# Issuing half of the memory keys' transfers from Scalar's queue in a one-core hybrid decoder layer

## The chip, the cores and the metric

The kernel runs as one program on one core of a Trainium2 chip. The metric is the device time of one execution in microseconds (us). A core has a TensorE (PE in the profile, with its weight loads as PEld), a VectorE (DVE), a ScalarE (ACT), a GpSimd (POOL) and a SyncE (SP). All of them run their own instruction rows in order and meet through semaphores. A transfer between the chip's memory and the on-chip buffers is issued by an instruction that stands in one of these rows (here SP's or ACT's) and is then carried out by the core's 16 DMA engines.

## The reference, cut to what matters

The reference computes one decoder layer for 512 prompt rows and for 8 samples of 4 rows: a mixer of two kinds of heads, a cross-attention into 256 memory tokens, and a gated MLP with a short convolution. The change touches the samples' cross-attention, whose keys and values come from a cache in memory:

```python
def mem_attend(h, mk, mv, w_mq, w_mo):
    B, T, _ = h.shape
    q = (h @ w_mq).reshape(B, T, MEM_HEADS, MEM_HEAD_DIM)
    s = jnp.einsum('bqhd,bkhd->bhqk', q.astype(jnp.float32), mk.astype(jnp.float32)) * (MEM_HEAD_DIM ** -0.5)
    p = jax.nn.softmax(s, axis=-1)
    o = jnp.einsum('bhqk,bkhd->bqhd', p, mv.astype(jnp.float32)).reshape(B, T, D_MODEL)
    return o.astype(h.dtype) @ w_mo
...
mem_attend(h, cache_mem_k[l], cache_mem_v[l], ...)   # samples: 8 x 256 tokens x 4 heads x 256, float32
```

## The kernel before

All products are float32 accuracy made of three passes: a number is split into a high part (a cast on ACT, L146) and the rest (a subtraction on DVE, L147), for weights (`wslot`, loaded through a staging tile `wst`) and activations alike.

The stretch around the change works as follows. The queries' projection (weights `w_mq`) makes eight chunks of 128 columns, numbered 0 to 7 here. Chunks 0 to 3 come first (L1428): the first halves of the four, then their second halves; chunks 4 to 7 follow (L1556), both halves of a chunk together. Each half is one PSUM tile `mm`, from a pool of five. It is emptied by ACT (`qh`, L1420), then DVE (`ql`, L1421), and a second half, which holds the samples' 32 columns, once more by ACT (`qs`, L1423); only then may TensorE take its buffer again. POOL spreads `qs` into `qx` (L1408).

Beside this, `mk_load` (L1488 to L1494) fetches a sample's memory keys: two tiles of 128 partitions per sample (c = 0, 1), each by four transfers, one a head, of 32 partitions and 128 KB. The eight samples make 64 transfers, 8.4 MB. Three samples of the first four use six staging tiles (`wst`), shared with the weights of the chunks 4 to 7; the others use weight slots or a free tile (`kvt`). `mk_turn` (L1498) lets DVE transpose each tile once its four transfers have landed. After all chunks, TensorE does part of the prompt's cross-attention (`sca`, L1441), the samples' scores (`ssc`, L1510) from `qx` and the transposed keys, and turns the prompt's softmax (`cpt`, L1459), which needs the softmax's last step on DVE (`cp`, L1450). The samples' values come after that (L1538).

The order on every engine is made by a scheduler when the program is built; so a change in one line can move instructions on several engines. Transfers use eight completion counters (DMAHW0 to DMAHW7 in the rows below), handed out in turn in the program's order whatever the queue: an issue waits until the transfer that held its counter before has landed. An instruction that waits holds up all that stands behind it in its engine's row, and that holds for a transfer's issue too.

Of the kernel before, what the change touches and what calls it, by code (L numbers as in the profile page):

```python
# [20 lines left out]
NS = NB * TS  # L21
# [56 lines left out]
def kernel(ctx: ExitStack, tc: tile.TileContext, I, O):  # L78
    nc = tc.nc
# [47 lines left out]
    def v2(t, b):  # L127
        return t.rearrange("p (a b) -> p a b", b=b)
# [10 lines left out]
    dma = nc.sync.dma_start  # L139
# [1070 lines left out]
    for b in range(4):  # L1210
        c = slice(b * P, b * P + P)
# [3 lines left out]
    kst, kts, pts, aTs, outs, rcs = {}, {}, {}, {}, {}, {}  # L1215
# [260 lines left out]
    kst, vts = {}, {}  # L1476
# [4 lines left out]
    def two(i):  # L1481

        if i < 3:
            return [stage(), stage()]
        t = wp.tile([P, 2, DM], F32, name="kvt", tag="W") if i < 7 else S([P, 2, DM], F32, "kvt")
        return [t[:, 0], t[:, 1]]

    def mk_load(b):  # L1488

        kst[b] = two(home[b])  # L1490
        for c in range(2):
            for h in range(H):
                dma(out=v2(kst[b][c][NS * h:NS * h + NS], 256),
                    in_=I["cache_mem_k"][0, b, c * P:(c + 1) * P, h].rearrange("(k t) d -> t k d", t=NS))  # L1494

    def mk_turn(b):
# [57 lines left out]
    for k in range(4):  # L1554
        mk_load(SEQS[k])
    for i, _ in enumerate(gemmB(hqT, [ev_q(m) for m in range(4, 8)])):  # L1556
        if i % 4 == 1:
            mk_turn(SEQS[i // 4])
        if i % 4 == 3:
            mk_load(SEQS[4 + i // 4])  # L1560
# [424 lines left out]
```

## Time and profile before

| | us |
|---|---|
| runs of the kernel | 952.9, 953.73, 956.4 (median 953.73) |
| profiled execution, whole | 950.42 |
| its span, first to last instruction | 948.6 |
| TensorE matmul busy in the span | 918.3 (97%) |
| DVE busy | 606.2 (64%) |
| ACT busy | 377.7 (40%) |

Times in the rows are microseconds from the span's start. A row of the timeline gives start, duration, engine and source line, what is written and read, how many instructions are merged (x), and in brackets how long the engine had been idle and which instruction or transfer ended that. A row on SPq or ACTq is the issue of a transfer, not the transfer. A row of the windows gives a stretch, its length, busy time and count of instructions of the five engines, the granted TensorE clock (1.00 is full), the busy share of the DMA engines, and GB/s moved.

### The profile page before, as it was taken

The page shows a single profiled execution, that of the slowest core. Times are in us where ns is not written, and L with a number is a line of the kernel's source. Part 1 is how long each engine was busy: PE and PEld are TensorE (multiplying, and loading weights), DVE is VectorE, ACT ScalarE, POOL GpSimd, SP SyncE. Part 2 cuts the span into 40 slices and gives each one's busy share as a digit, 9 for nine tenths or more (in the row PEclk, how much of TensorE's full clock was granted, in tenths as well). Part 3 has the DMA queues.
Part 4 walks back from the last instruction along what each step waited for, and adds up shares of the span by engine and source line. Part 5 has one row for each costly group of instructions (what it writes and reads, how often), then busy time and mean ns, then how long its engine had stood idle before and what let it go on. Part 6 is the DMA issues. An engine that isn't in the chain of part 4 may idle for free. (4 is left out here: it accounts for less than half of the span.)

```text
span 948.6 us, 17140 instructions
## 1 busy us (share of the span) xinstructions
PE 918.3 (97%) x6612; PEld 800.8 (84%) x6612; DVE 606.2 (64%) x1120; ACT 377.7 (40%) x727; POOL 202.6 (21%) x401
## 2 busy tenths in 40 slices
PE   8999999999999999988989999999999999999995
PEld 5899787889866778988767899989988997999974
DVE  6845145565886358576544778638757775676767
ACT  5655234344676357613434532322212222222232
POOL 6610000115432226301000544001110110110114
PEclk9999999999999999999989999999999999999998
DMA  8950023344870539999744733062053313512023
GB/s 285 309 183 2 2 88 137 89 139 131 280 245 9 176 103 343 262 192 260 273 175 124 208 126 89 25 174 72 8 142 100 102 27 92 153 49 89 24 93 116
DMA packets 127586, 130.30 MB, mean 137 GB/s; under 512 B 9336, under 2 KB 95193, under 8 KB 127505
## 3 DMA queue, kind: packets, MB, share of 16 engines
q1 hardware_dynamic: 121320, 125.70, 43.8%
q10 hardware_dynamic: 6184, 3.52, 1.2%
q8 instruction: 52, 0.85, 0.4%
q14 instruction: 30, 0.24, 0.1%
HBM read 112.26 MB, written 16.93 MB: 136 GB/s over the span
## 5 line engine op out<-in xcount | busy, mean ns | idle before, releaser
L485 PE MATMUL mm<-fT,wslot 128*128 128x256 f32 x1872 | 235.9, 288 | 0.0
L485 PEld LDWEIGHTS mm<-fT,wslot 128*128 128x128 f32 x1872 | 234.4, 188 | 1.8 <-issue 0.8
L146 ACT CAST wslot<-wst 128x1024 fp32r<-128x1024 f32 x125 | 130.7, 1050 | 256.7 <-issue 71.8
L147 DVE TENSOR_TENSOR wslot<-wst,wslot 128x1024 fp32r<-128x1024 f32 x125 | 155.2, 1246 | 83.3 <-ACT wslot L146 82.8
L1795 PE MATMUL mm<-wslot,act 128*128 128x512 f32 (+1 forms) x180 | 70.2, 391 | 0.0
L1796 PE MATMUL mm<-wslot,act 128*128 128x512 f32 (+1 forms) x180 | 70.0, 392 | 0.0
L1794 PE MATMUL mm<-wslot,act 128*128 128x512 f32 (+1 forms) x180 | 69.3, 387 | 0.0
L1700 POOL COPY cvo<-u 128x2 f32<-128x2 f32 x43 | 10.4, 243 | 204.0 <-DVE u L1698 194.0
L411 PE MATMUL mm<-wslot,hT 128*128 128x512 f32 x128 | 51.3, 402 | 0.0
L485 PE MATMUL mm<-hT,wslot 128*128 128x256 f32 (+1 forms) x384 | 51.0, 289 | 0.0
L413 PE MATMUL mm<-wslot,hT 128*128 128x512 f32 x128 | 51.0, 399 | 0.0
L412 PE MATMUL mm<-wslot,hT 128*128 128x512 f32 x128 | 50.8, 397 | 0.0
L1695 DVE TENSOR_TENSOR u<-mm,rsb 128x256 f32<-128x256 f32 x43 | 18.1, 423 | 50.1 <-PE mm L485 50.1
L485 PEld LDWEIGHTS mm<-hT,wslot 128*128 128x128 f32 x384 | 49.2, 188 | 0.5 <-issue 0.2
L1794 PEld LDWEIGHTS mm<-wslot,act 128*128 128x128 f32 x180 | 34.3, 191 | 8.0 <-issue 0.8
L1796 PEld LDWEIGHTS mm<-wslot,act 128*128 128x128 f32 x180 | 33.8, 188 | 7.3 <-issue 0.4
L1795 PEld LDWEIGHTS mm<-wslot,act 128*128 128x128 f32 x180 | 33.8, 188 | 7.2
L1712 ACT ACTIVATE c<-c 128x560 f32<-128x560 f32 x21 | 14.1, 672 | 57.0 <-DVE c L1706 57.0
L1706 DVE SCALAR_TENSOR_TENSOR c<-u,cvT,c 128x560 f32<-128x560 f32 x43 | 34.3, 797 | 0.9
L1705 DVE SCALAR_TENSOR_TENSOR c<-u,cvT,c 128x560 f32<-128x560 f32 x43 | 34.1, 793 | 0.2
L1807 DVE TENSOR_TENSOR yp<-mm,yp 128x512 f32<-128x512 f32 (+1 forms) x41 | 27.2, 674 | 5.2 <-PE mm L1796 5.1
L485 PE MATMUL mm<-hqT,wslot 128*128 128x256 f32 x192 | 26.2, 299 | 3.8 <-ACT qs L1423 3.8
(482 smaller groups left out, 1828.4 us busy)
## 6 DMA issues: line engine op xcount, KB each, us to landing
wst<-in_w_up_dram SPq DMA_DIRECT2D x42, 512.0 KB
wst<-in_w_in_dram SPq DMA_DIRECT2D x28, 512.0 KB
wst<-in_w_down_dram SPq DMA_DIRECT2D x20, 512.0 KB
kvt<-in_cache_mem_k_dram SPq DMA_DIRECT2D x40, 128.0 KB
kvt<-in_cache_mem_v_dram SPq DMA_DIRECT2D x10, 512.0 KB
wst<-in_w_mk_dram SPq DMA_DIRECT2D x8, 512.0 KB
xb<-in_x_prompt_dram SPq DMA_DIRECT2D x8, 512.0 KB
wst<-in_cache_dk_dram SPq DMA_DIRECT2D x16, 256.0 KB
```

The lines of the kernel that those rows point to most:

```text
L146: nc.scalar.copy(out=hi, in_=src)
L147: (eng or nc.vector).tensor_tensor(out=lo, in0=src, in1=f32(hi), op=SUB)
L411: mm(ps[b], lhsT=xt.hi(k, c0, c0 + n), rhs=s[:, 0, kk, :], start=(k == 0), stop=False)
L412: mm(ps[b], lhsT=xt.hi(k, c0, c0 + n), rhs=s[:, 1, kk, :], start=False, stop=False)
L413: return mm(ps[b], lhsT=xt.lo(k, c0, c0 + n), rhs=s[:, 0, kk, :], start=False, stop=(k == nk - 1))
L485: mm(ps[i], lhsT=s[:, l, k, :], rhs=x(k, c0, c1), start=(k == 0 and j == 0), stop=(k == 7 and j == 2))
L1705: STT(out=c, in0=u[:, 1:EXT - 1], scalar=w[1], in1=c, op0=MUL, op1=ADD)
L1706: STT(out=c, in0=u[:, 0:EXT - 2], scalar=w[0], in1=c, op0=MUL, op1=ADD)
L1794: mm(ps, lhsT=t[:, 0, c0:c0 + P], rhs=s[:, 0, i % 2, cs], start=st, stop=False)
L1795: mm(ps, lhsT=t[:, 0, c0:c0 + P], rhs=s[:, 1, i % 2, cs], start=False, stop=False)
L1796: return mm(ps, lhsT=t[:, 1, c0:c0 + P], rhs=s[:, 0, i % 2, cs], start=False, stop=en)
L1807: VTT(out=y, in0=ps, in1=y, op=ADD)
```

## The change

```diff
         kst[b] = two(home[b])
         for c in range(2):
             for h in range(H):
-                dma(out=v2(kst[b][c][NS * h:NS * h + NS], 256),
+                (dma, nc.scalar.dma_start)[h % 2](out=v2(kst[b][c][NS * h:NS * h + NS], 256),
                     in_=I["cache_mem_k"][0, b, c * P:(c + 1) * P, h].rearrange("(k t) d -> t k d", t=NS))
```

`dma` is SP's `dma_start`. Of every four transfers of a tile, those of heads 0 and 2 stay in SP's row, those of heads 1 and 3 go into ACT's. What is moved, how much, and where it lands stay as they were; 32 of the 64 issues change their row. TensorE's and POOL's orders are the same as before.

The first place is ACT's row where the second tile of values' weights is split (`mvN`), the first halves of chunks 2 and 3 are emptied (`qh`), and the weights of chunk 4 are cast (`wslot`). Names in brackets are the semaphores that an instruction waits for. Before:

```order
L146 CAST mvN<-wst 128x1024 [waits DMAHW2_49]
L1420 ACTIVATE qh<-mm 128x256 [waits DMAHW6_49,PE_49]
L1420 ACTIVATE qh<-mm 128x256 [waits PE_49]
L146 CAST wslot<-wst 128x1024 [waits DMAHW3_49,PE_49]
L1420 ACTIVATE qh<-mm 128x256
```

The same place on ACT now:

```order
L146 CAST mvN<-wst 128x1024 [waits DMAHW2_49]
L1493 DMA kvt<-in_cache_mem_k_dram 32x4x256
L1420 ACTIVATE qh<-mm 128x256 [waits DMAHW6_49,PE_49]
L1493 DMA wst<-in_cache_mem_k_dram 32x4x256 [waits DMAHW4_49,DVE_49]
L1493 DMA wst<-in_cache_mem_k_dram 32x4x256 [waits DMAHW6_49]
L1420 ACTIVATE qh<-mm 128x256 [waits PE_49]
L1493 DMA wst<-in_cache_mem_k_dram 32x4x256 [waits DMAHW0_49,DVE_49]
L1493 DMA wst<-in_cache_mem_k_dram 32x4x256 [waits DMAHW2_49]
L1493 DMA kvt<-in_cache_mem_k_dram 32x4x256 [waits DMAHW4_49]
L1493 DMA kvt<-in_cache_mem_k_dram 32x4x256 [waits DMAHW6_49]
L146 CAST wslot<-wst 128x1024 [waits DMAHW3_49,PE_49]
L1420 ACTIVATE qh<-mm 128x256
```

Eight issues (one more stands just ahead of these rows) have come in front of the cast of chunk 4's weights. The fourth of them takes its counter from the last of the four weight transfers of `w_mq` (DMAHW6), and the eighth takes its counter from the fourth.

The second place is ACT's row for the chunks 4 to 7, where before only the emptying of PSUM stood. Before, from chunk 4 to chunk 7:

```order
L1420 ACTIVATE qh<-mm 128x256 x2
L1423 ACTIVATE qs<-mm 128x32
L1420 ACTIVATE qh<-mm 128x256 x2
L1423 ACTIVATE qs<-mm 128x32
L1420 ACTIVATE qh<-mm 128x256 x2
L1423 ACTIVATE qs<-mm 128x32
L1420 ACTIVATE qh<-mm 128x256 x2
L1423 ACTIVATE qs<-mm 128x32
```

Now, from the `qs` of chunk 4 to the issues ahead of the `qs` of chunk 7:

```order
L1423 ACTIVATE qs<-mm 128x32
L1493 DMA kvt<-in_cache_mem_k_dram 32x4x256 x2
L1420 ACTIVATE qh<-mm 128x256 x2
L1493 DMA kvt<-in_cache_mem_k_dram 32x4x256 x3
L1423 ACTIVATE qs<-mm 128x32
L1493 DMA kvt<-in_cache_mem_k_dram 32x4x256
L1420 ACTIVATE qh<-mm 128x256 x2
L1493 DMA kvt<-in_cache_mem_k_dram 32x4x256 x2
L1423 ACTIVATE qs<-mm 128x32
L1493 DMA kvt<-in_cache_mem_k_dram 32x4x256 x2
L1420 ACTIVATE qh<-mm 128x256 x2
L1493 DMA kvt<-in_cache_mem_k_dram 32x4x256 x2
```

Behind the `qs` of chunks 4, 5 and 6 now stand two, one and two issues; they belong to the second tile (c = 1) of a sample, which DVE transposes before it does the next chunk's `ql`. The `qs` of chunk 7 and two last issues, for the last tile of all, follow these rows.

The third place is DVE's row from the low part of chunk 4's weights (the first `wslot`) to the `ql` of chunk 2's second half. Before:

```order
L147 TENSOR_TENSOR wslot<-wst,wslot 128x1024
L1421 SCALAR_TENSOR_TENSOR ql<-mm,qh 128x256
L1498 STREAM_TRANSPOSE wst<-wst 128x1024 x2
L1498 STREAM_TRANSPOSE kvt<-kvt 128x1024
L147 TENSOR_TENSOR wslot<-wst,wslot 128x1024
L1421 SCALAR_TENSOR_TENSOR ql<-mm,qh 128x256
L1498 STREAM_TRANSPOSE kvt<-kvt 128x1024
L1498 STREAM_TRANSPOSE wst<-wst 128x1024
L147 TENSOR_TENSOR wslot<-wst,wslot 128x1024
L1421 SCALAR_TENSOR_TENSOR ql<-mm,qh 128x256
```

The same place on DVE now:

```order
L1498 STREAM_TRANSPOSE kvt<-kvt 128x1024
L147 TENSOR_TENSOR wslot<-wst,wslot 128x1024
L1421 SCALAR_TENSOR_TENSOR ql<-mm,qh 128x256
L1498 STREAM_TRANSPOSE wst<-wst 128x1024
L147 TENSOR_TENSOR wslot<-wst,wslot 128x1024
L1498 STREAM_TRANSPOSE wst<-wst 128x1024
L1421 SCALAR_TENSOR_TENSOR ql<-mm,qh 128x256
L1498 STREAM_TRANSPOSE kvt<-kvt 128x1024
L1498 STREAM_TRANSPOSE wst<-wst 128x1024
L147 TENSOR_TENSOR wslot<-wst,wslot 128x1024
L1421 SCALAR_TENSOR_TENSOR ql<-mm,qh 128x256
```

The transpose of the first `kvt` tile has moved ahead of the low part of chunk 4's weights; what follows the `ql` of chunk 0's second half has one transpose less: three transposes of a key tile stood between that `ql` and the next low part of weights, now one does. Further on, DVE's last transpose of all has moved from behind the four `cp` steps (L1450) to ahead of them, and on SP, besides the 32 issues that left, some of the small convolution loads and of the values' loads have changed places among themselves.

## The prediction, as put on record before the run

> **What bounds the kernel.** TensorE is busy for 97% of the span, so I read first which waits of TensorE are left, and where. The list of waits, TensorE's own, longest first:
>
> ```profile
> PE mm L485 <- ACT qs L1423: 3.8, 2, 3.4
> ...
> PE ssc L1510 <- POOL qx L1408: 2.4, 1, 2.4
> ```
>
> Two of the three longest (total us, times, longest) lie in the stretch in which the memory keys are loaded. TensorE's timeline there:
>
> ```profile
> 403.51 6.15 PE L485 MATMUL mm<-hqT,wslot 128*128 128x256 f32 x48
> 410.07 0.38 PE L485 MATMUL mm<-hqT,wslot 128*128 128x256 f32 x1 [0.41 <-ACT qs L1423]
> 413.80 19.65 PE L485 MATMUL mm<-hqT,wslot 128*128 128x288 f32 x143 [3.35 <-ACT qs L1423]
> ...
> 436.01 0.28 PE L1441 MATMUL sca<-mkT,ql 128*128 128x256 f32 x1
> 438.71 3.57 PE L1510 MATMUL ssc<-wst,qx 128*32 128x128 f32 x95 [2.42 <-POOL qx L1408]
> ...
> 443.20 0.66 PE L1459 MATMUL cpt<-cpk,cp 128*128 128x128 f32 x4
> ```
>
> Chunk 4 runs from 403.51, chunk 5 cannot start properly before 413.80, and the samples' scores cannot start before 438.71: 3.76 and 2.42 us of idle TensorE. That is what there is to win or to make worse; from 443.20 on TensorE runs on, and a shift there goes through to the end. Who holds these waits is on DVE:
>
> ```profile
> 395.18 1.23 DVE L147 TENSOR_TENSOR wslot<-wst,wslot 128x1024 fp32r<-128x1024 f32 x1 [0.86 <-ACT wslot L146]
> 396.33 0.42 DVE L1421 SCALAR_TENSOR_TENSOR ql<-mm,qh 128x256 fp32r<-128x256 f32 x1
> 403.45 1.25 DVE L1498 STREAM_TRANSPOSE wst<-wst 128x1024 f32<-128x1024 f32 x1 [6.71 <-DMA wst<-in_cache_mem_k_dram]
> 405.97 1.25 DVE L1498 STREAM_TRANSPOSE wst<-wst 128x1024 f32<-128x1024 f32 x1 [1.27 <-DMA wst<-in_cache_mem_k_dram]
> ...
> 413.10 0.41 DVE L1421 SCALAR_TENSOR_TENSOR ql<-mm,qh 128x256 fp32r<-128x256 f32 x1
> ...
> 418.15 1.25 DVE L1498 STREAM_TRANSPOSE wst<-wst 128x1024 f32<-128x1024 f32 x1 [2.04 <-DMA wst<-in_cache_mem_k_dram]
> 419.32 0.72 DVE L1421 SCALAR_TENSOR_TENSOR ql<-mm,qh 128x256 fp32r<-128x256 f32 x2
> ```
>
> DVE waits 6.71 us for the first keys, and the `ql` that `qs` needs stands behind. And ACT:
>
> ```profile
> 394.10 1.05 ACT L146 CAST wslot<-wst 128x1024 fp32r<-128x1024 f32 x1 [1.15 <-PE mm L472]
> ...
> 413.55 0.20 ACT L1423 ACTIVATE qs<-mm 128x32 f32<-128x32 f32 x1 [2.32 <-DVE ql L1421]
> 420.07 0.20 ACT L1423 ACTIVATE qs<-mm 128x32 f32<-128x32 f32 x1 [3.17 <-DVE ql L1421]
> ...
> 438.17 0.20 ACT L1423 ACTIVATE qs<-mm 128x32 f32<-128x32 f32 x1 [3.96 <-DVE ql L1421]
> ```
>
> So the chain is: keys land, transpose, `ql`, `qs`, a PSUM buffer (or `qx`), TensorE. Is the issue of the keys the limit? Rows of SP's issues, then of stretches:
>
> ```profile
> 395.56 1.81 SPq L1493 DMA_DIRECT2D wst<-in_cache_mem_k_dram x4
> ...
> 399.33 0.31 SPq L1493 DMA_DIRECT2D wst<-in_cache_mem_k_dram x1
> ...
> 413.21 1.73 SPq L1493 DMA_DIRECT2D wst<-in_cache_mem_k_dram x4
> ...
> 420.00:426.00 6.00, 6.00 (x50) 6.00 (x50) 3.16 (x4) 0.86 (x3) 0.00 (x0) 1.00 1.14 215
> ...
> 442.00:448.00 6.00, 6.00 (x165) 5.67 (x158) 3.72 (x9) 3.06 (x10) 0.00 (x0) 1.00 0.98 388
> ```
>
> Four issues take 1.73 us, 0.43 each. At 215 GB/s a transfer of 131,072 bytes takes 0.61 us, and the engines are full (share 1.14). Issuing is faster than carrying, so a second issuer by itself brings nothing; what counts is when each issue comes, and what waits behind it.
>
> **The cost of an issue, and of a landing.** ACT already issues such transfers elsewhere, and the median (the middle number, ns) is
>
> ```profile
> L555 ACTq DMA_DIRECT2D mk_d<-mkT x4: 366/372/384, 42.0 to 55.0; - x4
> ...
> 403.00:414.00 11.00, 7.23 (x56) 6.82 (x55) 9.28 (x10) 1.61 (x4) 0.91 (x4) 1.00 0.74 167
> ```
>
> I take 0.4 us, with SP's 0.43. The 32 issues are 12.8 us of ACT's row between 389 and 439, where ACT has room (1.61 of 11 us busy in the stretch shown); the room hides the durations. It doesn't hide the waits. How long after its issue a transfer can be used, L, is not shown alone. From the row at 413.21, the fourth issue began at 413.21 + 1.73 - 0.43 = 414.51, and the transpose that waited began at 418.15: 3.6 us. With the three others' share taken off (the first began at 413.21: 4.94 us, less 4 x 0.61, leaves 2.5 fixed), one alone would need 2.5 + 0.6 = 3.1. The other end is the full queue: the four from 395.56 ended at 397.37, so the last began at 396.94, and were used at 403.45: 6.5 us. I take **L = 3.6**, from the row nearest to it: four or five transfers in flight.
>
> **First place: the cast of chunk 4's weights.** ACT's fourth issue needs the counter of the last `w_mq` transfer. SP's ninth keys' issue waited for the same counter and began at 399.33. So the fourth issue goes at 399.33; `qh` and three more issues stand behind it (0.4 each, until 400.9); the eighth needs the fourth's landing, 399.33 + 3.6 = 402.9, and ends at 403.3. Only then comes the cast that stood at 394.10: until 404.35. The low part follows on DVE at 404.4 (1.1 us to the next), `ql` at 405.5, and the next transpose at 405.85. From there to the `ql` of chunk 2 stand the same eight instructions (four transposes, two low parts, two `ql`) as from 405.97 to 413.10, so that `ql` starts at 413.0, and its `qs`, behind one issue that waits for a staging tile freed at 413.1, runs at 413.5. Chunk 5 then starts at 413.75, as before (413.80). What changes is chunk 4: its second half needs the PSUM buffer that the `qs` of chunk 0 frees, behind the ninth issue, at 406.55. Chunk 4 starts then, 3.1 us late, and ends at 412.7, ahead of chunk 5's gate. The later cast is covered by the wait that the transposes made: **0**. Without that cover it would cost the 3.1 us.
>
> **Second place: the rounds of chunks 4 to 7.** After chunk 2's `qs` one issue goes at 413.7 and lands by 417.3, where the transpose of 418.15 can start; two `ql` (0.72) and the `qs` of chunk 4 follow at 419.25 (before: 420.07). Now a round: `qs` 0.2, the second of two issues begins 0.4 later, lands 3.6 later, transpose 1.16, two `ql` 0.72: 6.1 us to the next `qs`; with one issue 5.7. Chunk 7's `qs` comes at 419.25 + 6.1 + 5.7 + 6.1 = 437.15, against 438.17. The scores follow 0.54 later (438.17 to 438.71 in the rows): 437.7, **1.0 us earlier**. TensorE could be there at 436.3 at the latest (its work of 413.80 to 436.29 starts 0.05 earlier), so it is not the limit.
>
> **Third place: the softmax.** The last two issues stand behind chunk 7's `qs`; the second begins at 437.75, lands at 441.35, and DVE's last transpose, now ahead of `cp`, ends at 442.6. Two `cp` steps take
>
> ```profile
> 440.82 1.51 DVE L1450 TENSOR_SCALAR cp<-cp,csu 128x256 f32<-128x256 f32 x4
> ```
>
> half of 1.51, so `cpt` starts at 443.35. Without the wait it would start 438.71 to 443.20, that is 4.49 us, after the scores, at 442.2. So the 1.0 us is given back, and 0.15 more.
>
> **The sum.** 0 - 1.0 + 1.15 = +0.15 us at TensorE's turn at 443. SP loses 32 issues, which gives nothing (it was ahead of the carriers), and its values' loads wait for scores to be read, so they move with the scores; the changed places among the small convolution loads and the values I cost at nothing, since TensorE does not wait for either before; if that cover went, one late values' load would cost about one landing, 3.6 us. Against the profiled execution (950.42) that gives 950.6; the median of the runs shown is 953.73, 0.35% higher, and I put the sum on it: **953.9 us**. L enters six times (the eighth issue, the one at 413.7, three rounds, the last transpose): each 0.1 us of L is 0.6 us. L = 3.1 gives 0.15 - 3.0 = -2.9 (950.9), L = 6.5 gives 0.15 + 17.4 = +17.5 (971).
>
> **Rivals.** *Slower: ACT's issues meet full queues.* Eight keys' transfers a round are 8 x 0.61 = 4.9 us of carrying in a round of 5.7 to 6.1, so the queues are never far from full; SP issues its four as soon as a chunk ends, and ACT's last two come behind them. From L = 4.5 on, the loss is over 5 us; at L = 5, (5 - 3.6) x 6 + 0.15 = +8.5 us: **962**. For it speaks the wait of 6.71; against it, that this came behind the four weight transfers of `w_mq`, and the row at 413.21. Its mark is that each round is over 6.9 us.
>
> *Faster: two queues carry more.* Tiles of 32 partitions move at 215 GB/s, full-height values at 388. If the two heads in flight from two queues reached 388, a transfer would take 0.34 us and L = 2.5 + 0.34 = 2.8: 0.15 - 4.8 = -4.6, **949**. The Trainium skill ("SBUF — State Buffer", section "Door 1: The DMA port swizzle") says that partitions 0 to 63 reach only one half of the 16 ports and 64 to 127 the other; our 215 against 388 agrees, and by it heads 0 and 1 share a half and heads 2 and 3 share one, so the gain would come only while the queues are on different halves. Its section "Can I just issue two DMAs to hit both halves?" reports only 6% from two at once; by that L would fall by 0.04 and the time by 0.2 us, and I give this case little.
>
> There is also TensorE's clock:
>
> ```profile
> 414.00:420.00 6.00, 6.00 (x37) 6.00 (x37) 3.96 (x6) 0.75 (x3) 0.92 (x4) 0.72 0.96 212
> ```
>
> After the 3.35 us gap the clock was 0.72 over 6 us, 1.7 us of work lost. In the forecast TensorE isn't the limit at 438, so this counts only in the fast case, where it would lower the floor from 436.3 to 434.6 if the gaps (3.1 and 1.0 now) are too short for a drop.
>
> **Chances.** Forecast (within 0.5%, 949.0 to 958.5, which is about what a measurement of this kernel can tell from no change): L between 2.8 and 4.4, 0.59. Slow rival: 0.28. Fast rival or more: 0.13. The median could also move by its own scatter of 0.35%. The range that leaves out two in ten goes from the fast case to the slow one: 948.5 to 963. What lies above (L over 5.1, up to the 971 of the full queue) I give 0.12, what lies below 0.08.
>
> **What would show it.** Right: the cast of chunk 4's weights moves from 394 to about 403; TensorE waits 3 us before chunk 4 and 1 us before chunk 5; rounds between `qs` of about 6 us; scores near 437.7 and `cpt` waiting for `cp`. Wrong: keys used over 4.5 us after ACT's issue (slow), or GB/s well over 215 from 420 to 432 with rounds down at TensorE's 5.9 us a chunk (fast); or waits of TensorE after 445 that were not there before, for values or convolution loads, which I cost at nothing.

## The result, and the profile after

| | before | changed |
|---|---|---|
| median of 11 runs, us | 953.77 (950.96 to 956.63) | 957.31 (954.98 to 960.57) |
| ratio of the times, 95% interval | | 1.0042 [1.0023, 1.0061] |
| profiled execution, whole, us | 950.42 | 954.98 |

The changed kernel is slower by 0.42% (0.23 to 0.61), about 4.0 us (3.5 between the medians). The 957.31 lies inside the range on record (948.5 to 963) and within its bound of 0.5%, but the interval excludes no change: the forecast of 953.9 missed 3.4 us that are real. That it lies inside says little for the working, since the range is wider than the effect. Three executions in the experiments below, of 1122, 2317 and 3186 us, are slow ones and stand in no ratio.

From the page of the changed kernel, its span and the busy time of TensorE:

```profile
span 953.2 us, 17144 instructions
...
PE 919.8 (96%) x6612; PEld 803.1 (84%) x6612; DVE 606.2 (64%) x1120; ACT 377.5 (40%) x727; POOL 202.6 (21%) x401
```

The other engines are as busy as before. The span is 4.6 us longer; TensorE is busy 1.5 us more of it and idle 3.1 us more. Its waits now, longest first (total us, times, longest):

```profile
PE ost L1595 <- ACT oS L1592: 4.9, 1, 4.9
PE ssc L1510 <- POOL qx L1408: 4.4, 1, 4.4
...
```

The waits of the stretch in TensorE's timeline of the changed kernel:

```profile
385.12 18.02 PE L472 MATMUL mm<-hqT,wslot 128*128 128x256 f32 x138
...
405.17 0.38 PE L485 MATMUL mm<-hqT,wslot 128*128 128x256 f32 x1 [2.03 <-ACT wslot L146]
407.07 19.68 PE L485 MATMUL mm<-hqT,wslot 128*128 128x288 f32 x144 [1.52 <-ACT qs L1423]
428.24 6.14 PE L485 MATMUL mm<-hqT,wslot 128*128 128x288 f32 x47 [1.49 <-DVE ql L1421]
...
441.58 4.42 PE L1510 MATMUL ssc<-wst,qx 128*32 128x128 f32 x95 [4.36 <-POOL qx L1408]
446.91 0.66 PE L1459 MATMUL cpt<-cpk,cp 128*128 128x128 f32 x4
```

The wait ahead of chunk 5 is gone, and two at chunk 4 have taken its place: 2.03 + 1.52 = 3.55 us, for 3.76 before. There TensorE has lost nothing. It loses later: 1.49 us in chunk 7, behind its first matmul (1 + 144 of the 192 of chunks 4 to 7 are done; the second half's buffer is one that the `ql` of chunk 5 empties), 4.36 instead of 2.42 ahead of the scores, and `cpt` comes at 446.91 instead of 443.20. ACT's timeline shows which step is late:

```profile
396.25 5.29 ACTq L1493 DMA_DIRECT2D wst<-in_cache_mem_k_dram  x2
...
404.07 1.04 ACT L146 CAST wslot<-wst 128x1024 fp32r<-128x1024 f32 x1 [2.10 <-DMA wst<-in_cache_mem_k_dram]
...
420.23 0.20 ACT L1423 ACTIVATE qs<-mm 128x32 f32<-128x32 f32 x1 [1.87 <-DVE ql L1421]
...
428.55 0.20 ACT L1423 ACTIVATE qs<-mm 128x32 f32<-128x32 f32 x1 [5.99 <-DVE ql L1421]
...
434.51 0.20 ACT L1423 ACTIVATE qs<-mm 128x32 f32<-128x32 f32 x1 [4.93 <-DVE ql L1421]
434.52 0.84 ACTq L1493 DMA_DIRECT2D kvt<-in_cache_mem_k_dram  x2
...
441.03 0.20 ACT L1423 ACTIVATE qs<-mm 128x32 f32<-128x32 f32 x1 [4.97 <-DMA kvt<-in_cache_mem_k_dram]
```

The two rows of before that the prediction didn't show, the `qs` of chunks 5 and 6:

```profile
427.29 0.20 ACT L1423 ACTIVATE qs<-mm 128x32 f32<-128x32 f32 x1 [5.25 <-DVE ql L1421]
...
433.47 0.20 ACT L1423 ACTIVATE qs<-mm 128x32 f32<-128x32 f32 x1 [5.38 <-DVE ql L1421]
```

Step by step, as changes against before in us (a round is the time from one chunk's `qs` to the next one's):

| step | before | changed | change | predicted change |
|---|---|---|---|---|
| `qs` of chunk 4, at | 420.07 | 420.23 | +0.16 | -0.82 |
| first round (to chunk 5) | 7.22 | 8.32 | +1.10 | -1.12 |
| second round (to chunk 6) | 6.18 | 5.96 | -0.22 | -0.48 |
| third round (to chunk 7) | 4.70 | 6.52 | +1.82 | +1.40 |
| `qs` of chunk 7 to scores | 0.54 | 0.55 | +0.01 | 0 |
| scores to `cpt` | 4.49 | 5.33 | +0.84 | +1.16 |
| sum, at `cpt` | 443.20 | 446.91 | +3.71 | +0.14 |

The table counts from the starts of the spans. Chunks 0 to 3 start on TensorE at 385.65 before and at 385.12 now; counted from there, the `qs` of chunk 4 is 0.69 us late, not 0.16, and `cpt` 4.24, not 3.71.

So two places cost time, the stretch up to the `qs` of chunk 5 and the third round, and the gain that was expected at chunk 4 and in the first round didn't come.

**The first round** is late because of the DMA engines. SP's issues in the changed kernel, and behind them SP's wait in the stretch 409 to 418 that before doesn't have:

```profile
416.80 0.79 SPq L1493 DMA_DIRECT2D wst<-in_cache_mem_k_dram  x2
```

```profile
SPq L1493 <- DVE wslot L147: 1.4, 1, 1.4
```

Before, the issues at this place in SP's row:

```profile
415.04 1.80 SPq L1493 DMA_DIRECT2D wst<-in_cache_mem_k_dram  x4
```

They fill the staging tile that the low part of chunk 7's weights has just been read from. DVE's rows of that low part and of the transpose beside it, in the changed kernel, then before:

```profile
414.42 1.25 DVE L1498 STREAM_TRANSPOSE wst<-wst 128x1024 f32<-128x1024 f32 x1 [0.26 <-DMA wst<-in_cache_mem_k_dram]
415.59 1.18 DVE L147 TENSOR_TENSOR wslot<-wst,wslot 128x1024 fp32r<-128x1024 f32 x1
```

```profile
413.44 1.21 DVE L147 TENSOR_TENSOR wslot<-wst,wslot 128x1024 fp32r<-128x1024 f32 x1
414.57 1.24 DVE L1498 STREAM_TRANSPOSE wst<-wst 128x1024 f32<-128x1024 f32 x1
```

Before, the tile was free at 413.44 + 1.21 = 414.65, ahead of the issue. Now it is free at 416.77, and the issue waits for that. The low part is 2.15 us later. Some 0.64 of this is DVE's row running late behind the late cast (the `ql` of chunk 2 starts at 413.74, before at 413.10). The other 1.5 is the transpose, which the scheduler has put ahead of it, with its own wait for keys. The profiles of E1, E3, E5, E9 and E12 below, which have the eight issues too, show this order on DVE; those of E2, E4 and E10, which don't, show the order of before. So those runs move the cast and this order together and don't tell the two apart. The DMA view of the stretch 412 to 424, in 40 slices of 0.3 us, first the changed kernel, then before:

```profile
GB/s 225 178 82 27 27 24 0 0 0 99 140 266 352 280 253 225 130 3 0 133 89 17 283 382 280 225 222 208 198 212 256 191 198 212 232 198 208 205 253 191
DMA packets 2202, 2.01 MB, mean 168 GB/s; under 512 B 245, under 2 KB 2201, under 8 KB 2201
```

```profile
GB/s 208 167 116 72 14 0 0 20 242 365 256 171 225 229 205 219 191 232 202 208 236 236 208 195 219 242 208 198 219 232 219 205 208 222 222 205 205 219 236 195
DMA packets 2525, 2.30 MB, mean 192 GB/s; under 512 B 279, under 2 KB 2525, under 8 KB 2525
```

Both pause near 414. The changed kernel's engines run mostly dry again from 417.1 to 418.6, and carry 0.29 MB less in the stretch. At 215 GB/s that is 1.35 us, and the `qs` of chunk 5 is 1.26 us later (1.79 from the start of chunks 0 to 3).

**The third round** is late by ACT's issues at 434.52: they come only when the `qs` of chunk 6 has run. Before, SP had issued all eight transfers of that sample by 432.2; its row, and then the transpose in the changed kernel that waits for the two:

```profile
427.49 4.74 SPq L1493 DMA_DIRECT2D kvt<-in_cache_mem_k_dram  x8
```

```profile
439.12 1.25 DVE L1498 STREAM_TRANSPOSE kvt<-kvt 128x1024 f32<-128x1024 f32 x1 [3.08 <-DMA kvt<-in_cache_mem_k_dram]
```

The second of them began at about 434.9 and was used at 439.12: L = 4.2 us. Last, the scores run after 4.36 us of idle TensorE. The window of the changed kernel behind them (stretch, length, busy time of PE, PEld, DVE, ACT and POOL, granted clock, DMA share, GB/s):

```profile
442.00:448.00 6.00, 6.00 (x136) 5.58 (x135) 3.82 (x9) 3.68 (x13) 2.14 (x3) 0.81 0.73 229
```

TensorE is as busy as before, but at a clock of 0.81 instead of 1.00 it does 136 matmuls in these 6 us instead of 165: that is how I read the +0.84 from scores to `cpt`.

### The profile page after: what moved, and what is told of

It reads as the page before. It is cut to its first block, busy times and chain, and to the rows that moved or that the text cites. A ratio compares the mean times of both kernels' runs of the same rounds, so it can differ in the third digit from the quotient of the medians.

```text
span 953.2 us, 17144 instructions
## 1 busy us (share of the span) xinstructions
PE 919.8 (96%) x6612; PEld 803.1 (84%) x6612; DVE 606.2 (64%) x1120; ACT 377.5 (40%) x727; POOL 202.6 (21%) x401
```

## The experiments

Times are medians, ratios stand against runs of the kernel before beside them on the same chip (its medians were 953.32, 953.82 and 953.81 in the three groups E1 to E4, E5 to E8, E9 to E12). A ratio of 1.001 is 0.95 us.

My theory was that the time goes in two places of ACT's row: at the issues ahead of chunk 4's cast, and at those behind the `qs` of the late chunks. The rivals were that only one of the two counts, that the loss lies in how the transfers are carried (which heads are neighbours, and in how many queues), and that it is the transposes' place on DVE that turns a late key into a wait of TensorE.

### E1 to E3: which samples' transfers cost the time

Each is the changed kernel with the split for some samples only, in the order of loading (SEQS). E1 splits the first four:

```diff
-                (dma, nc.scalar.dma_start)[h % 2](out=...
+                (dma, nc.scalar.dma_start)[h % 2 * (b in SEQS[:4])](out=...
```

E2 splits the last four, E3 the first six:

```diff
+                (dma, nc.scalar.dma_start)[h % 2 * (b in SEQS[4:])](out=...     (E2)
+                (dma, nc.scalar.dma_start)[h % 2 * (b in SEQS[:6])](out=...     (E3)
```

> Only the first four samples' keys (32 of the 64 transfers) are split between SP and ACT; the second four stay in SP's row. Theory A (two separate costs: the first place starves the DMA engines at 414 to 417 because a staging tile of chunk 7's weights comes free about 2 us later, which makes the qs of chunk 5 about 1.2 us later; and ACT's issues behind the qs of chunk 6 make the last round 1.8 us longer): here only the first cost is left. The qs of chunk 5 at about 428.5 (before 427.29), the round from the qs of chunk 6 to that of chunk 7 back at 4.7 to 5.0 us, the scores 1 to 1.5 us later than before, the kernel +1 to +2 us. Rival B (everything comes from ACT issues behind qs): qs of chunk 5 at 427.3, no change (within 0.5 us). Rival C (the late cast of chunk 4's weights costs its full 3.1 us): +3 us or more.

> Only the second four samples' keys are split; the first four stay in SP's row, so the first place is as before. Theory A: qs of chunk 5 as before (427.3, within 0.3), the last round (qs of chunk 6 to qs of chunk 7) 6.5 us instead of 4.7, the scores 1.5 to 2 us later, a gap of TensorE before them of about 4 us and a lower clock behind it; the kernel +2 to +3 us. Rival B (all from ACT's issues behind qs): about the whole +3.5 us. Rival D (the loss came from the first place alone): 0.

> The first six samples' keys are split, the last two samples' stay in SP's row (no issue behind the qs of chunk 6 belongs to a tile that the qs of chunk 7 waits for). Theory A: like the first four alone: qs of chunk 5 about 428.5, the last round back at 4.7 to 5.0, the kernel +1 to +2 us. Rival E (ACT's issues lengthen every round in which they stand): the rounds of chunks 5 and 6 stay long as in the changed kernel and the last one too, since everything in it starts later: +2.5 to +3.5 us.

| | us | ratio | rounds 1, 2, 3 |
|---|---|---|---|
| E1, first four | 955.21 | 1.0010 [0.9996, 1.0024] | 7.82 6.68 4.78 |
| E2, last four | 954.65 | 1.0013 [0.9999, 1.0028] | 7.47 5.90 6.60 |
| E3, first six | 954.31 | 1.0010 [0.9997, 1.0024] | 7.81 6.77 3.39 |

In time none of the three can be told from no change by itself. In the traces they part: the first round is the longer one (7.8, against 7.47 in E2) where the first samples are split, the last one is long (6.60) where the last two are. The `qs` of chunks 6 and 7 in E2, and the same two in E3:

```profile
432.86 0.20 ACT L1423 ACTIVATE qs<-mm 128x32 f32<-128x32 f32 x1 [4.37 <-DMA kvt<-in_cache_mem_k_dram]
439.46 0.20 ACT L1423 ACTIVATE qs<-mm 128x32 f32<-128x32 f32 x1 [5.02 <-DMA kvt<-in_cache_mem_k_dram]
```

```profile
437.60 0.20 ACT L1423 ACTIVATE qs<-mm 128x32 f32<-128x32 f32 x1 [5.73 <-DVE ql L1421]
440.99 0.20 ACT L1423 ACTIVATE qs<-mm 128x32 f32<-128x32 f32 x1 [2.64 <-DVE ql L1421]
```

With the last two samples' issues back on SP the third round falls to 3.39, further than I expected. So the third round's loss belongs to ACT's issues for the last two samples. The ratios point the same way: E3's edit differs from the change in these 16 issues alone, and its interval ends at 1.0024, where that of the changed kernel begins (1.0023; run again, 1.0021).

### E4 and E5: is it the queue, or which heads are neighbours?

E4 leaves all issues on SP, but in the order of heads 0, 2, 1, 3, so that neighbours write to different halves of the 128 partitions. Against the kernel before:

```diff
-            for h in range(H):
+            for h in (0, 2, 1, 3):
```

E5 keeps two queues, with heads 0 and 1 on SP, 2 and 3 on ACT:

```diff
-                (dma, nc.scalar.dma_start)[h % 2](out=...
+                (dma, nc.scalar.dma_start)[h // 2](out=...
```

> All 64 transfers in SP's row as before, but of each tile the heads in the order 0, 2, 1, 3, so that neighbouring transfers go to different halves of the partitions. If the halves of the ports were what limits the keys to 215 GB/s (the faster rival of the prediction): over 250 GB/s in the stretch 420 to 426, the qs of chunk 5 ahead of 426.5, scores 2 us earlier, the kernel -2 to -4 us. If each transfer of 131,072 bytes takes its 0.61 us wherever its neighbours go: 215 GB/s, and no change within 0.5 us.

> As the changed kernel, 32 transfers on ACT, but heads 2 and 3 go to ACT and heads 0 and 1 stay with SP, so that the two queues write to different halves of the partitions at a time. Theory A with the finding on the order 0, 2, 1, 3 (neighbours in one half slow each other): transfers land about 0.5 us apart instead of 0.6 in the rounds of chunks 5 and 6, the round of chunk 5 comes down to 6.5 to 7 us (8.3 in the changed kernel), but the last round still has ACT's two issues behind the qs of chunk 6 and stays over 6 us: the kernel between before -1 and before +2 us. Rival F (it is the second queue itself that costs, whichever half): like the changed kernel, +3.5 us.

E4 took 949.77 us, ratio 0.9958 [0.9943, 0.9974]: faster than before, by the order alone. Its profile is of the slowest of its eight runs (953.91), and the scores come only 1.0 us earlier there than before, counted from the start of chunks 0 to 3, where 2 were expected; so the gain stands in the times, and where it is won isn't shown. E5 took 955.97, 1.0018 [1.0008, 1.0028]. The windows of E4 and of before over the same six microseconds:

```profile
416.00:422.00 6.00, 6.00 (x33) 6.00 (x33) 3.88 (x6) 0.95 (x4) 0.92 (x4) 0.61 1.03 238
...
420.00:426.00 6.00, 6.00 (x48) 6.00 (x47) 4.00 (x5) 0.86 (x3) 0.00 (x0) 0.94 0.87 214
```

```profile
416.00:422.00 6.00, 6.00 (x44) 6.00 (x43) 3.25 (x5) 1.57 (x6) 0.92 (x4) 0.86 1.10 216
```

The same engines, no busier, carry 10% more. From 420 to 426 E4 shows 214, not the 250 and more that I looked for, since its issues run out there (share 0.87). E5 over that stretch, then the changed kernel:

```profile
420.00:426.00 6.00, 6.00 (x51) 6.00 (x50) 3.60 (x5) 0.85 (x3) 0.00 (x0) 1.00 1.11 240
```

```profile
420.00:426.00 6.00, 6.00 (x51) 6.00 (x50) 2.69 (x3) 0.86 (x3) 0.00 (x0) 1.00 1.15 215
```

So in this stretch two queues carry more when they work on different halves, and not when they work on the same one (from 426 to 432 E5 shows 210 at a share of 1.00, so the 240 is not lasting). In this change head 1 goes beside head 0 and head 3 beside head 2, and it stays at 215. E5's faster carrying shortens its last rounds (7.47, 5.20, 5.37; I had expected a first round of 6.5 to 7 and a last one above 6), and it is still slower than before: the split takes back more than the halves give.

### E6 to E8: the chain from the transposes to TensorE, taken away

In the kernel before, the transposes wait on DVE ahead of the `ql` that TensorE's buffers need. E6 is the kernel before with each sample's transposes put behind a later step of DVE:

```diff
-            mk_turn(SEQS[i // 4])
+            with tc.issue_after(qd[(3, 3, 4, 4)[i // 4]].ins):
+                mk_turn(SEQS[i // 4])
...
-    for k in range(4, 8):
-        mk_turn(SEQS[k])
+    for k, d in zip(range(4, 8), (qd[5], qd[6], rd[1], cd[1])):
+        with tc.issue_after(d.ins):
+            mk_turn(SEQS[k])
```

Here `qd[m]` is the `ql` of chunk m, `rd[1]` and `cd[1]` are steps of the prompt's softmax (L1444, L1450). E7 is E6 with E4's order of heads, E8 is the changed kernel with the same hold.

> All transfers in SP's row as before; DVE's transposes are held back: those of the first two samples behind the ql of chunk 3, the next two behind the ql of chunk 4, then one sample each behind the ql of chunk 5, the ql of chunk 6, the prompt's reductions and the last cp step. No ql stands behind a transpose that waits for keys. Theory A (keys, transpose, ql, qs, PSUM buffer is the chain that makes TensorE wait): the waits of 3.35 us before chunk 5 and of 2.42 us before the scores are gone or under 1 us, the clock does not drop at 414 to 420, the kernel -3 to -7 us. Rival G (TensorE waits for the keys themselves, so that the wait only moves to the scores): the scores of the first or second four samples start no earlier and wait 3 us or more, the kernel -1 to +1 us.

> Both: SP's row with the heads in the order 0, 2, 1, 3, and the transposes held back as in the kernel with the held transposes. Theory A: once no ql waits for keys, faster keys are worth little more: as that kernel, or up to 2 us less where the second four samples' scores still wait. Rival G: the two gains add up, a further 4 us less.

> The changed kernel (heads 1 and 3 issued by ACT) with the same transposes held back. Theory A (ACT's issues cost time because a tile that lands late holds the ql behind it): with no ql behind a waiting transpose the split costs little: within 1.5 us of the kernel with SP's row and held transposes, and faster than before by 2 us or more. Rival H (ACT's issues cost by what stands behind them on ACT: the cast of the weights at 404, qh and qs): the 3.5 us of the split stay, so 3 to 4 us above the kernel with SP's row and held transposes.

| | us | ratio |
|---|---|---|
| E6, SP alone, held | 947.83 | 0.9944 [0.9927, 0.9961] |
| E7, 0 2 1 3, held | 947.02 | 0.9930 [0.9916, 0.9944] |
| E8, split, held | 950.74 | 0.9970 [0.9959, 0.9982] |

In E6 TensorE is busy through the chunks, and its clock stays full; its windows from 403 to 420, and then the one wait that is left at the scores:

```profile
403.00:414.00 11.00, 11.00 (x90) 11.00 (x89) 6.94 (x8) 2.39 (x6) 0.92 (x4) 1.00 0.97 223
414.00:420.00 6.00, 6.00 (x51) 6.00 (x50) 4.56 (x6) 0.86 (x3) 0.00 (x0) 1.00 1.12 231
```

```profile
441.07 1.08 PE L1510 MATMUL ssc<-kvt,qx 128*32 128x128 f32 x32 [1.33 <-issue]
```

So in the kernel before it is the transposes' place ahead of `ql` that makes TensorE wait for keys. E7 carries 252 GB/s where E6 carries 231 (the times of the two can't be told apart, their intervals overlap):

```profile
414.00:420.00 6.00, 6.00 (x50) 6.00 (x49) 3.78 (x6) 0.86 (x3) 0.00 (x0) 1.00 0.98 252
```

In E8 the chain is gone as well, and the split still costs 2.9 us against E6 (0.9970 against 0.9944; the two intervals just touch). Its TensorE at chunk 4:

```profile
406.24 0.38 PE L485 MATMUL mm<-hqT,wslot 128*128 128x256 f32 x1 [2.17 <-ACT wslot L146]
408.14 26.63 PE L485 MATMUL mm<-hqT,wslot 128*128 128x288 f32 x191 [1.52 <-ACT qs L1423]
```

That is 3.69 us of waits for the late cast and for the `qs` behind the issues, with nothing to hide them. The 2.9 us are nearer to the 3 to 4 that rival H asked for than to theory A's 1.5. But they are lost at chunk 4, where the changed kernel loses nothing, so E8 shows what ACT's row costs without cover; how much of the changed kernel's own loss goes through the transposes, it doesn't show.

### E9 to E12: the two places apart, and the two kernels again

E9 moves to ACT only what stands ahead of the cast (the eight issues of the first sample and the fourth), E10 only the second, third, fifth and sixth samples' (16 issues, none ahead of the cast, none for the last two samples):

```diff
+                (dma, nc.scalar.dma_start)[h % 2 * (b in (SEQS[0], SEQS[3]))](out=...            (E9)
+                (dma, nc.scalar.dma_start)[h % 2 * (b in SEQS[1:3] + SEQS[4:6])](out=...      (E10)
```

E11 is the kernel before, for one more profile, and E12 the changed kernel, both without an edit.

> Only the keys of the first and the fourth sample are split: the eight issues of ACT that stand ahead of the cast of chunk 4's weights are there, and DVE's order is that of the changed kernel up to chunk 4; no other issue moves. Theory A (first place): the cast stands at 404 to 406 instead of 395, the low part of chunk 7's weights comes 2 us or more later, the DMA engines move under 180 GB/s from 414 to 420, and the kernel loses what the kernel with the first four samples' keys loses, +1 to +2 us. Rival J (these eight issues are covered by DVE's wait for the first keys, as predicted): within 0.5 us of before.

> The keys of the second, third, fifth and sixth sample are split, 16 issues on ACT, none of them ahead of the cast of chunk 4's weights and none behind the qs of chunk 6; DVE's order is that of before. Theory A (the cost sits in these two places): no change, within 1 us of before. Rival K (every issue on ACT behind a qs costs its share): half of 3.5 us, +1.8 us.

> The kernel of before once more, for a second profile: how far single profiled executions scatter in the rounds of chunks 4 to 7. If the comparison of rounds is sound, the rounds between the qs of chunks 4 to 7 come again within 0.5 us each (7.2, 6.2 and 4.7 us) and the DMA engines move over 200 GB/s in the 6 us behind the qs of chunk 2.

> The changed kernel once more, for a second profile. Theory A: rounds of about 8.3, 6.0 and 6.5 us again (the last over 6), TensorE waits over 3.5 us before the scores; 3 to 4 us over before. If the first profile was a chance one, the last round is nearer to 4.7 us.

| | us | ratio | `qs` of chunk 5, from the start of chunks 0 to 3 | rounds 1, 2, 3 |
|---|---|---|---|---|
| before | 953.77 | | 41.64 | 7.22 6.18 4.70 |
| E11, before again | 954.11 (one run) | | 40.79 | 7.27 6.37 5.11 |
| changed | 957.31 | 1.0042 [1.0023, 1.0061] | 43.43 | 8.32 5.96 6.52 |
| E12, changed again | 957.36 | 1.0038 [1.0021, 1.0056] | 44.06 | 7.59 6.15 6.11 |
| E9, first place only | 954.66 | 1.0007 [0.9990, 1.0023] | 43.99 | 7.33 6.43 4.70 |
| E10, middle only | 953.19 | 0.9995 [0.9972, 1.0018] | 41.13 | 7.40 7.75 3.09 |

The fourth column is counted from TensorE's row at 385.12 in the changed kernel and its like in the others, since their spans start a little apart. It parts the kernels cleanly: 43.2 to 44.1 with the eight issues ahead of the cast (E1, E3 and E5 are 43.98, 44.03 and 43.18), 39.9 to 41.6 without (E2 40.47, E4 39.91). E9's cast, and its low part of chunk 7's weights, which frees the staging tile:

```profile
406.09 1.04 ACT L146 CAST wslot<-wst 128x1024 fp32r<-128x1024 f32 x1 [2.15 <-DMA wst<-in_cache_mem_k_dram]
```

```profile
417.67 1.18 DVE L147 TENSOR_TENSOR wslot<-wst,wslot 128x1024 fp32r<-128x1024 f32 x1
```

Its DMA engines move 2.02 MB from 412 to 424, like the changed kernel's 2.01; E10's move 2.33, like before's 2.30. In E12 the loss of some 2 us stands mostly ahead of chunk 4's `qs` rather than in the first round (7.59, where I expected 8.3); at chunk 5's `qs` it is the same. E9's first round (7.33) is no longer than before's either: what this place moves is the `qs` of chunk 5, not one round. E11's DMA engines carry 198 GB/s in the 6 us behind the `qs` of chunk 2, just under the 200 looked for.

E10 shows what a late issue costs when there is a later round to make it up. There a tile carried by ACT's issues is late in the second round (7.75), and the transpose waits:

```profile
434.33 1.25 DVE L1498 STREAM_TRANSPOSE kvt<-kvt 128x1024 f32<-128x1024 f32 x1 [3.94 <-DMA kvt<-in_cache_mem_k_dram]
```

but the third takes 3.09, as SP's transfers for it have landed meanwhile: both together 10.84, before 10.88, and the time is that of before (its interval reaches up to 1.7 us, so rival K's 1.8 is excluded only just). In the changed kernel and in E2 the two take 12.5.

The profiled executions lie up to 4 us from the medians (E4's at 953.91 for 949.77, before's at 950.42 for 953.77), so they show places, and the ratios show sizes. E9's is one of its two slowest runs (957.10): there `cpt` comes 3.7 us later than before, counted from the start of chunks 0 to 3, nearly as much as in the changed kernel, while the median is higher by 0.9 only. By the ratios the first place alone (E9) is not told from zero, E1 and E2 together give 0.23%, and the whole gives 0.40%. The intervals overlap; whether the two places cost more together than apart stays open.

## Why the prediction was right and wrong

**First place, right on TensorE's row, wrong on its price.** The cast came at 404.07 (predicted 403.3), chunk 4 with its second half at 407.07 (406.55), and no wait was left ahead of chunk 5, where the prediction left 1 us. So far "the later cast is covered by the wait that the transposes made" held. E8 takes that cover away, and 3.69 us of waits appear (I had put 3.1 on it). The step that failed is the **0**. I followed the late cast along TensorE, and stopped at chunk 5. The path ran on through DVE: the low parts of the chunks 4 to 7 free the staging tiles that the next keys land in. That this place moves chunk 5's `qs` by 2 to 3 us is shown by E9 and E10 on either side. That the staging tile passes it on is read from the rows of the changed kernel and of E9, and no run takes the tile alone away. Nor does one take the late cast without the transpose that moved ahead of chunk 7's low part, which makes 1.5 of the 2.15 us: the prediction compared DVE's orders only as far as the `ql` of chunk 2, and this stands just behind.

**Second place, rounds sized by the wrong quantity.** "A round: 6.1 us" was built from L, the latency of one late issue. But three tiles are transposed between chunk 4's `qs` and chunk 5's, 12 transfers, and 12 x 0.61 = 7.3 us of carrying: the round took 7.22 before, 7.40 in E10. At that rate of carrying no earlier issue could have brought the 1.12 us that the sum took from it, nor did the 0.82 ahead of it come. I had the price of a transfer, and used it only for rounds of eight. These two (0.82 + 1.12 not gained, 0.16 + 1.10 lost) make 3.2 of the 3.57 us by which the sum failed. The third round was the right mechanism with a small error: +1.82 for +1.40, as L was 4.2 instead of 3.6. In the sum its +1.40 stood hidden behind gains of 2.42, of which 0.22 came.

**Third place, right size, wrong cause.** `cpt` doesn't wait for `cp`, which ran at 445.29, and TensorE worked through from the scores to `cpt`. The +0.84 goes with the lower clock after the gap, which the prediction priced only for the fast case. That its size is near the +1.16 is luck: the stretch from the scores to `cpt` took some 4.5 us in E3, E4 and E10, as before, and some 6.15 in E1, E2 and E5.

**What I costed at nothing.** Of values and convolution loads no new wait shows. TensorE's wait at `ost` (4.9 after, 3.4 before) is no sign of it: the kernel before, profiled again, has 6.12 there.

```profile
484.63 0.69 PE L1595 MATMUL ost<-cpk,oS 128*128 128x128 f32 x2 [6.12 <-ACT oS L1592]
```

But this wait breaks a premise of the prediction: "from 443.20 on TensorE runs on, and a shift there goes through to the end". It was the second longest of the waits before (3.4), and it ends with `oS`, which stands on ACT behind casts of the weights of `w_mo`, and these wait for their transfers. ACT's row of the cast just ahead of `oS` in the changed kernel:

```profile
484.95 1.04 ACT L146 CAST wslot<-wst 128x1024 fp32r<-128x1024 f32 x1 [0.51 <-DMA wst<-in_w_mo_dram]
```

E6 shows what that does: counted from the start of chunks 0 to 3, its `cpt` comes 9.1 us earlier than before, its `ost` only 4.1, after the longest such wait:

```profile
478.19 0.69 PE L1597 MATMUL ost<-cpk,oS 128*128 128x128 f32 x2 [7.48 <-ACT oS L1594]
```

So a shift at `cpt` is not yet a shift of the time, and only the ratios say what is left of it.

**The rivals.** The slow one asked for rounds over 6.9 us and L above 4.5; the rounds were 8.32, 5.96 and 6.52, the first for another reason, and L 4.2. The fast one's 949 went below the prediction's own floor: with the scores at 436.3 at the earliest, or at 434.6, 2.4 or 4.1 of its 4.6 us could be won. Of the fast one the premise is true for other pairs of heads, as E4 and E5 show, and void for this change: 215 GB/s as before. I gave it little because of the 6% that the Trainium skill reports ("SBUF — State Buffer", section "Can I just issue two DMAs to hit both halves?"). That figure sets two transfers at once against a single one; neighbours in different halves against neighbours in one give more here: 10 to 12% between the pairs shown above (238 for 216, 240 for 215), and a kernel faster by 0.42%.

## What to carry to other kernels

An issue that is moved to another engine's row costs little by itself; price what it waits for there, what stands behind it, and follow that to the release of the buffer that the next transfers need, not only to the busiest engine. A late transfer is made up when a later round has slack, and lost when it is the last one. What paid here lay beside the change: keep steps that may wait for transfers out of the row ahead of what frees TensorE's buffers (E6, -0.56%), and let neighbouring narrow transfers go to different halves of the partitions (E4, -0.42%); both together are E7, 947.02 us, 0.9930 [0.9916, 0.9944], which is not their sum and can't be told from E6 alone.

## What the runs showed of the hardware that was not expected

The halves of the partitions count between transfers that follow each other in one queue, too: the order 0, 2, 1, 3 raised 216 GB/s to 238 without a second queue. That agrees with the Trainium skill ("DMA: Bandwidth & Descriptors", section "Issuing engines are not separate DMA queues"), by which a second issuer saves only the time of issuing: two queues (E5, 240) carried no more than one in a good order.

TensorE's clock fell after shorter gaps than looked for, in one profile after a very short one. In E5 TensorE waited 2.21 us ahead of the scores, and the window behind it has a clock of 0.55:

```profile
440.69 5.24 PE L1510 MATMUL ssc<-wst,qx 128*32 128x128 f32 x95 [2.21 <-POOL qx L1408]
```

```profile
442.00:444.00 2.00, 2.00 (x49) 2.00 (x45) 1.81 (x3) 1.30 (x6) 1.37 (x1) 0.55 0.50 112
```

The kernel before, with 2.42 us, and again with 2.83, ran the same scores in 3.57 us:

```profile
439.49 3.57 PE L1510 MATMUL ssc<-wst,qx 128*32 128x128 f32 x95 [2.83 <-POOL qx L1408]
```

The other profiles keep an order: 3.57 us for these scores after waits of 2.03 and 2.26 us (E3, E10), and 4.42 to 5.24 after waits of 3.01 to 4.36 (E9, E1, E2, E12 and the changed kernel); E5 alone falls out of it. So the length of one gap doesn't settle it here. The Trainium skill ("TensorE: Matmul & The Clock Gate", section "Part 1: The HAM clock gate") speaks of an idle window of about 3.4 us; the drops in E5, E9 (3.01) and E1 (3.32) came with less idle time just ahead of them than that, and what else counted is open.
